# First tokens read once, later sums made tile by tile, and twelve sums of each stage on VectorE

## The chip, the core and the metric

The kernel runs on one core of a Trainium2 chip. The core has TensorE (PE in the profile; PEld is its weight load), VectorE (DVE), ScalarE (ACT), GpSimd (POOL) and SyncE (SP, which here only issues DMAs), each with its own queue of instructions that runs in order. The metric is the device time of one execution in microseconds (us), lower is better, as the median of several runs.

## The reference

One layer works on 1024 tokens of 1024 channels in float32: a feed-forward block (ffn1), a mixer (a short convolution beside a gated delta rule), a second feed-forward block (ffn2), a last norm. Each of the three blocks begins with the same two steps, an RMS norm and a wide matmul:

```python
def rmsnorm(x, w, eps=NORM_EPS):
    xf = x.astype(jnp.float32)
    y = xf * lax.rsqrt(jnp.mean(xf * xf, axis=-1, keepdims=True) + eps)
    return (y * w.astype(jnp.float32)).astype(x.dtype)
...
def swiglu_ffn(x, w_in, w_out):
    gate, up = jnp.split(x @ w_in, 2, axis=-1)
    return (jax.nn.silu(gate) * up) @ w_out
...
    h = h + 0.5 * swiglu_ffn(rmsnorm(h, ffn1_norm[layer]), ffn1_w_in[layer], ffn1_w_out[layer])
    u = rmsnorm(h, mix_norm[layer]) @ w_mix_in[layer]
```

## The kernel before

**Tiles.** The activations lie transposed, channels on the 128 partitions: `h[hf][d]` is a tile of 128 channels by 512 tokens, `hf` the half of the tokens (first, second) and `d` one of eight groups of channels. A product in float32 accuracy is three matmuls (`mm3`, L192 to L194): each operand is split into a high and a low part, and hi*hi, hi*lo and lo*hi are summed in PSUM. The high part is a copy on ACT (L103), the low part a subtraction on DVE (L104). For weights the parts are called `whi` and `wlo`, for activations `hi` and `lo`. One product of a 512x128 block of weights with a 512x512 block of activations is four `mm3`, so 12 matmuls of 512 columns.

**Strassen-Winograd.** A `Pair` takes two column blocks of a weight matrix, 2x2 blocks B11 to B22, against the 2x2 blocks A11, A12, A22 of the activations, in seven products in place of eight. That needs sums on both sides: of the weights, T1 = B12 - B11, T2 = T1 - B22, T3 = B22 - B12, T4 = B21 + T2 (`tsum`, `prep_p6`); of the activations, S1, nS2, S3, S4 (`Blocks.sums`, in three parts), for which the second half's tokens have to be normed. Before the change all T and the S4 were made on POOL through `pool_tt` (L111), the other S on DVE.

**The order at the start of a stage.** A stage here is the beginning of ffn1, of the mixer's projections (mix) or of ffn2. PE first does the "heads" of five early pairs: `head1` (B11 with A11), then `head2` (B21 with A12). These need the first half's tokens alone. Then come, for the first two pairs together, the products with S1 and nS2 (`both(k)`, k = 0 to 3: 2 pairs x 2 products x 3 = 12 matmuls for each k), then heads of later pairs between the products P7, P4 and P3. Work is given out as tasks of (load, prep, run), with loads 9 and preps 4 tasks ahead of the run (`run_tasks`); the framework's scheduler then orders DVE's instructions by its own plan, except those inside `keep_in_program_order`. `later(n, f)` calls f after n more `mm3`. `x.sums(0, ...)` made all four S1 and nS2 in one go, as soon as the second half's norm factor was spread (`spread`, a transpose on PE at L246 that puts one factor per token into all partitions).

**The beginning of ffn1.** `first_heads` read the tokens of the first half twice: as rows (`xtok`, 8 tiles of 256 KB, tokens on partitions), squared on ACT with a running sum for each token (`by_tokens`, L235), and as `xT` for the product. The factor is a power -0.5 on POOL (L220), which like the transposes needs the constants tile `cs`. `cs` was loaded on ACT's queue; `mask` (L783, L784) is cast from it on DVE. The second half was read as rows and as `xT` after that. The weights of the small projection `wba` were loaded and split at this point too (L745 to L749), though they are used only in the mixer.

Of the kernel before, what the change touches and what calls it, by code (L numbers as in the profile page):

```python
# [57 lines left out]
def tile_hybrid(  # L58
# [54 lines left out]


    tasks, done_to = [], [0, 0, 0]

# [39 lines left out]
    nc.scalar.activation(out=early, in_=early, func=AF.Square)  # L156

    ident = cs[:, C_ID:C_ID + P]
# [45 lines left out]
    class Norm:  # L204
# [24 lines left out]

        def by_tokens(self, src):  # L230

            tot = const.tile([P, 8], F32, name="tot", tag="tot", bufs=2)
            for i, tile_ in enumerate(src):
                tc.keep_in_program_order(
                    nc.scalar.activation(out=tile_, in_=tile_, func=AF.Square, accum_out=tot[:, i:i + 1]))  # L235
            tv = tot.rearrange("p (b i) -> p b i", i=2)
            both = const.tile([P, 4], F32, name="both", tag="both", bufs=2)
            nc.vector.tensor_tensor(out=both, in0=tv[:, :, 0], in1=tv[:, :, 1], op=ALU.add)
            self.factor(both)
# [28 lines left out]
    class Blocks:  # L268
# [3 lines left out]
        def __init__(self, h, which):  # L272
            self.h, self.g = h, V_N[which]
            self.s4 = []
            self.b = {n: [None] * KH for n in ("A11", "A12", "S1", "nS2", "S3", "S4", "A22")}
# [12 lines left out]
        def begin2(self, k):  # L288
# [5 lines left out]
                                           op0=ALU.mult, op1=ALU.add)  # L294

        def sums(self, part, rb):

            h, b = self.h, self.b
            if part == 0:
                for k in range(KH):  # L300
                    s1, s2 = h[1][k], h[0][k]
                    nc.vector.tensor_tensor(out=s1, in0=s1, in1=rb, op=ALU.mult)
                    nc.vector.tensor_tensor(out=s2, in0=s2, in1=s1, op=ALU.subtract)  # L303
                    b["S1"][k] = split(s1, slot)
                    b["nS2"][k] = split(s2, slot)
            if part == 1:
                for k in range(KH):
                    a22, s2 = h[1][k + KH], h[0][k]
                    nc.vector.scalar_tensor_tensor(out=a22, in0=a22, scalar=self.gain(k + KH), in1=rb,
                                                   op0=ALU.mult, op1=ALU.mult)  # L310
                    s4 = temp(F32, "s4")
                    self.s4.append(s4)
                    pool_tt(s4, h[0][k + KH], s2, ALU.add)
                    nc.vector.tensor_tensor(out=s2, in0=s2, in1=a22, op=ALU.add)
                    b["S3"][k] = split(s2, slot)
            if part == 2:
                for k in range(KH):
                    b["A22"][k] = split(h[1][k + KH], slot)
                for k in range(KH):
                    b["S4"][k] = split(self.s4[k], slot)  # L320

    class Pair:
# [5 lines left out]
        def __init__(self, x, srcs, first, done):  # L328
            self.x, self.srcs, self.first, self.done = x, srcs, first, done
            self.r, self.t, self.w, self.pinned = {}, {}, {}, False  # L330

# [48 lines left out]
        def body(self):  # L380
# [6 lines left out]
            def prep_p6():  # L387
                t["T1"] = tt_tile("T1")
                pool_tt(t["T1"], r["B12"], r["B11"], ALU.subtract)
                self.tsum("T2", t["T1"], r["B22"], ALU.subtract)  # L390
# [34 lines left out]
    def all_pairs(pairs, x, norm2, between={}, twos=(0, 2)):  # L425
# [214 lines left out]
    with ExitStack() as stack:  # L640
# [3 lines left out]

        def by_tokens(hf):
            tiles = []
            for b in range(KH):
                for i in range(2):
                    tiles.append(slot(F32, "xtok"))
                    tc.keep_in_program_order(nc.sync.dma_start(out=tiles[-1], in_=xtok[hf, b][:, i, :]))  # L650
            return tiles

        def get_x(hf, *ds):
# [3 lines left out]
        def first_heads(pairs):  # L657
            early = pairs[:EARLY]
            four = early[:4]
            for p in early:  # L660
                p.pinned = True
            rows1 = by_tokens(0)
            for k in range(KH):
                get_x(0, k)
                early[k].get("B11")
            get_x(0, *range(KH, KT))
            norms[0].by_tokens(rows1)
            norms[0].spread()
# [4 lines left out]
            def first(k):  # L673
                x.norm1(norms[0].rb, k)
                x.split1(k)

            def run(k):
# [3 lines left out]
                if k == KH - 1:  # L681
                    for p in four:
                        p.w.pop("B11")
                        p.copy_p1()

            for k in range(KH):
                first(k)
            rows2 = []

            def then():  # L690
                for d in range(KH, KT):
                    first(d)
                norms[1].by_tokens(rows2)

            def then2():
                for k in range(KH):
                    x.begin2(k)

            for k in range(KH):
                task(lambda k=k: run(k))  # L700
            task(*early[4].head1())
            task(*early[0].head2())
            task(None, then, lambda: rows2.extend(by_tokens(1)))
            task(*early[1].head2())
            task(None, None, lambda: get_x(1, 0, 4, 1, 5))
            task(*early[2].head2())
            task(norms[1].spread, then2, lambda: get_x(1, 2, 6, 3, 7))
            task(*early[3].head2())
            task(*early[4].head2())

# [5 lines left out]

        def t1_done():
            for d in range(KT):
                nm[0].square(d)
                nc.sync.dma_start(out=h_dr[0][d], in_=acc[0][d])  # L720
# [861 lines left out]
```

## Time and profile before

| | us |
|---|---|
| median of three runs (1858.66, 1865.97, 1868.80) | 1865.97 |
| the profiled execution's own time | 1864.1 |
| its span, first to last instruction | 1862.4 |
| granted TensorE clock over the span, share of full | 0.989 |

The page of the profile gives, for each engine, its busy time; a page's groups give line, engine, operation, output<-inputs, shapes, count, then busy time, mean length of one in ns, and the idle time before them with what ended it. In a timeline row stand the start, the length, the engine, the line, the operation and the tiles, and in brackets the idle time of that engine just before and what released it. In a row of windows stand the window, its length, each engine's busy time with the number of instructions that touch the window, the granted clock, the DMA engines' share and rate. An instruction on DVE is 0.68 us long in a timeline, but the next starts before its end.

### The profile page before, as it was taken

Reading aid. Unit: us, or ns where it says so; the run is one execution under the profiler, and the core shown is the slowest. Engines: PE = TensorE matmul, PEld = TensorE weight load, DVE = VectorE, ACT = ScalarE, POOL = GpSimd, SP = SyncE. Lnnn points to the kernel's source line nnn. Section 1 sums busy time; section 2 is a strip of 40 time slices with the busy share of each in tenths; the row PEclk is TensorE's granted clock in tenths of the full one; section 3 lists DMA queues with packets and bytes.
Section 4 is the critical chain, followed back from the end, with each engine's and each line's share of the span. In section 5 each row is a group of like instructions: output and inputs, shape, how many; then the busy total and the mean of one; then the engine's idle time right before and its main releaser. Section 6 shows DMA issues by size and latency. Waiting matters only on the chain.

```text
span 1862.4 us, 24801 instructions
## 1 busy us (share of the span) xinstructions
PE 1793.7 (96%) x8448; PEld 1464.3 (79%) x8448; DVE 1304.6 (70%) x1997; ACT 751.3 (40%) x1520; POOL 731.4 (39%) x514
## 2 busy tenths in 40 slices
PE   6899999999999999999989999999999999999997
PEld 4688888888888877777778887778888888888886
DVE  5976666667665887877867665878665666677666
ACT  6422323223534554468343344443222323244443
POOL 2474455445341432324322102045544454445243
PEclk9999999999999999999999999999999999999998
DMA  8144344435984542478744385522434344488642
GB/s 296 57 153 141 114 141 137 135 120 197 321 273 142 167 145 90 142 229 276 241 136 153 109 284 170 194 88 97 168 116 141 114 140 138 158 286 280 215 141 92
DMA packets 196238, 313.48 MB, mean 168 GB/s; under 512 B 28048, under 2 KB 50576, under 8 KB 196112
## 3 DMA queue, kind: packets, MB, share of 16 engines
q1 hardware_dynamic: 192656, 306.60, 49.9%
q10 hardware_dynamic: 3456, 5.31, 0.9%
q8 instruction: 66, 1.08, 0.2%
q14 instruction: 60, 0.49, 0.1%
HBM read 228.97 MB, written 82.86 MB: 167 GB/s over the span
## 4 chain that ended last, share of the span: by engine, by line
PE 78%; DVE 10%; ACT 4%; DMA 3%; issue 3%; POOL 1%; SPq 0%; ACTq 0%; POOLq 0%; DVEq 0%
PE ps_ps L194 22%; PE ps_ps L192 22%; PE ps_ps L193 22%; PE ps_mm L192 2%; PE ps_mm L194 2%; PE ps_mm L193 2%; DVE wlo L104 2%; DVE lo L104 1%; PE ps_aux L938 1%; DMA raw<-w_in 1%; DVE cv L842 1%; DVE sv L1092 1%; DVE xb L1096 1%; ACT whi L103 1%; DVE h L303 1%
## 5 line engine op out<-in xcount | busy, mean ns | idle before, releaser
L192 PE MATMUL ps_ps<-hi,whi 128*128 128x512 f32 x1400 | 550.1, 394 | 10.6 <-ACT hi L103 3.2
L194 PE MATMUL ps_ps<-hi,wlo 128*128 128x512 f32 x1400 | 548.5, 392 | 9.0 <-DVE wlo L104 9.0
L193 PE MATMUL ps_ps<-lo,whi 128*128 128x512 f32 x1400 | 549.0, 392 | 2.9 <-DVE lo L104 2.9
L104 DVE TENSOR_TENSOR wlo<-T,whi 128x512 fp32r<-128x512 f32 x244 | 228.8, 952 | 144.9 <-ACT whi L103 144.3
L104 DVE TENSOR_TENSOR wlo<-raw,whi 128x512 fp32r<-128x512 f32 x280 | 251.6, 909 | 102.3 <-ACT whi L103 100.5
L192 PEld LDWEIGHTS ps_ps<-hi,whi 128*128 128x128 f32 x1400 | 264.7, 189 | 72.0 <-ACT whi L103 4.7
L194 PEld LDWEIGHTS ps_ps<-hi,wlo 128*128 128x128 f32 x1400 | 264.9, 189 | 66.9 <-DVE wlo L104 11.7
L111 POOL TENSOR_TENSOR T<-raw 128x512 f32<-128x512 f32 x144 | 222.8, 1548 | 234.8 <-DVE wlo L104 102.5
L193 PEld LDWEIGHTS ps_ps<-lo,whi 128*128 128x128 f32 x1400 | 265.0, 189 | 60.3 <-DVE lo L104 5.6
L192 PE MATMUL ps_ps<-ghi,whi 128*128 128x512 f32 x616 | 241.3, 392 | 0.0
L194 PE MATMUL ps_ps<-ghi,wlo 128*128 128x512 f32 x616 | 240.8, 391 | 0.4 <-DVE wlo L104 0.4
L193 PE MATMUL ps_ps<-glo,whi 128*128 128x512 f32 x616 | 240.6, 391 | 0.0
L103 ACT CAST whi<-raw 128x512 fp32r<-128x512 f32 x280 | 169.2, 617 | 62.7 <-DMA raw<-w_in 23.0
L103 ACT CAST whi<-T 128x512 fp32r<-128x512 f32 x244 | 146.3, 616 | 76.1 <-PE ps_ps L193 33.1
L104 DVE TENSOR_TENSOR glo<-raw,ghi 128x512 fp32r<-128x512 f32 x154 | 128.7, 836 | 50.9 <-ACT ghi L103 48.2
L192 PE MATMUL ps_mm<-hi,whi 128*128 128x512 f32 x384 | 159.8, 416 | 3.8 <-ACT whi L103 2.7
L194 PE MATMUL ps_mm<-hi,wlo 128*128 128x512 f32 x384 | 152.7, 398 | 1.3 <-DVE wlo L104 1.3
L193 PE MATMUL ps_mm<-lo,whi 128*128 128x512 f32 x384 | 152.3, 397 | 0.0
L111 POOL TENSOR_TENSOR T<-raw,T 128x512 f32<-128x512 f32 x50 | 72.4, 1449 | 167.1 <-DMA raw<-w_in 127.5
L194 PEld LDWEIGHTS ps_ps<-ghi,wlo 128*128 128x128 f32 x616 | 115.7, 188 | 26.8 <-DVE wlo L104 1.3
L193 PEld LDWEIGHTS ps_ps<-glo,whi 128*128 128x128 f32 x616 | 115.9, 188 | 25.3
L192 PEld LDWEIGHTS ps_ps<-ghi,whi 128*128 128x128 f32 x616 | 115.7, 188 | 25.3
(223 smaller groups left out, 2230.7 us busy)
## 6 DMA issues: line engine op xcount, KB each, us to landing
raw<-w_in SPq DMA_DIRECT2D x264, 256.0 KB, 4.6
raw<-w_out SPq DMA_DIRECT2D x154, 256.0 KB, 4.2
raw<-w_qkv SPq DMA_DIRECT2D x36, 256.0 KB, 3.4
f1S<-S SPq DMA_DIRECT2D x33, 256.0 KB, 5.0
raw<-f1A SPq DMA_DIRECT2D x33, 256.0 KB, 3.9
raw<-f1S SPq DMA_DIRECT2D x33, 256.0 KB, 3.7
f2S<-S SPq DMA_DIRECT2D x33, 256.0 KB, 4.9
raw<-f2A SPq DMA_DIRECT2D x33, 256.0 KB, 4.4
```

Source lines behind the costliest of these rows:

```text
L103: tc.keep_in_program_order(nc.scalar.copy(out=hi, in_=src))
L104: nc.vector.tensor_tensor(out=lo, in0=src, in1=hi.bitcast(F32), op=ALU.subtract)
L111: tc.keep_in_program_order(nc.gpsimd.tensor_tensor(out=out, in0=in0, in1=in1, op=op))
L192: nc.tensor.matmul(out=ps, lhsT=whi, rhs=xhi, start=start, stop=False, skip_group_check=True)
L193: nc.tensor.matmul(out=ps, lhsT=whi, rhs=xlo, start=False, stop=False, skip_group_check=True)
L194: nc.tensor.matmul(out=ps, lhsT=wlo, rhs=xhi, start=False, stop=stop, skip_group_check=True)
L303: nc.vector.tensor_tensor(out=s2, in0=s2, in1=s1, op=ALU.subtract)
L842: nc.vector.scalar_tensor_tensor(out=acc, in0=u[:, i:i + HALF], scalar=vcol(wc + i), in1=acc, op0=ALU.mult, op1=ALU.add)
L938: nc.tensor.matmul(out=ps[:, sl], lhsT=lhs[:, sl], rhs=rhs[:, sl], start=start, stop=stop)
L1092: nc.vector.tensor_tensor(out=tv, in0=lrow[:, lo:hi].unsqueeze(2).broadcast_to([nb, n, j + 1]), in1=xrow[:, 0:j + 1].unsqueeze(1).broadcas ...
L1096: nc.vector.tensor_tensor(out=xv, in0=xv, in1=tv, op=ALU.subtract)
```

## The change

- `first_heads` loads the eight `xT` tiles of the first half first, then `cs` (now on SP's queue), then four weight blocks, the rows of the second half, its `xT` tiles, then the other weights. The rows of the first half aren't read at all.
- `as_they_land` takes the first half's sums from `xT`: ACT squares each tile, DVE adds two tiles at a time, PE sums over the channels by four matmuls with a column of ones, four times, into one PSUM bank.
- The second half's rows are squared one by one between the first half's splits (`row_square`), and its factor is spread right after the first 48 matmuls.
- `sums(0)` makes the first S1 and nS2, and gives the other three to `later` (4, 8 and 12 `mm3` on); `both(k)` asks for its own with `need(k)`.
- S4 in `sums(1)` and all T of the first two pairs go to DVE, in every stage: 4 + 8 sums of 128x512.
- `wba` is loaded and split at the end of ffn1's output product T1 (`split_ba`).

```diff
+    def dve_tt(out, in0, in1, op):
+        nc.vector.tensor_tensor(out=out, in0=in0, in1=in1, op=op)
...
     cs = const.tile([P, NCONST], F32, name="cs")
-    nc.scalar.dma_start(out=cs, in_=cst)
...
+        def as_they_land(self):
+
+            cp = psum(self.bank)
+            for j in range(KH):
+                two = [slot(F32, "sq") for _ in range(2)]
+                for i, sq in enumerate(two):
+                    tc.keep_in_program_order(
+                        nc.scalar.activation(out=sq, in_=self.hh[2 * j + i], func=AF.Square))
+                nc.vector.tensor_tensor(out=two[0], in0=two[0], in1=two[1], op=ALU.add)
+                for b in range(4):
+                    tc.keep_in_program_order(
+                        nc.tensor.matmul(out=cp[:, b:b + 1], lhsT=two[0][:, b * P:(b + 1) * P], rhs=one,
+                                         start=(j == 0 and b == 0), stop=(j == KH - 1), skip_group_check=True))
+            self.factor(cp[:, 0:4])
...
+        def need(self, k):
+            while self.b["S1"][k] is None:
+                self.pending.pop(0)()
...
             if part == 0:
-                for k in range(KH):
-                    s1, s2 = h[1][k], h[0][k]
...
+                self.pending = [lambda k=k: first(k) for k in range(KH)]
+                self.need(0)
+                for k in range(1, KH):
+                    later(SUM_STEP * k, lambda k=k: self.need(k))
...
-                    pool_tt(s4, h[0][k + KH], s2, ALU.add)
+                    nc.vector.tensor_tensor(out=s4, in0=h[0][k + KH], in1=s2, op=ALU.add)
...
-            pool_tt(self.t[n], p, q, op)
+            self.tt(self.t[n], p, q, op)
...
+        for p in pairs[:2]:
+            p.tt = dve_tt
...
-            rows1 = by_tokens(0)
-            for k in range(KH):
-                get_x(0, k)
-                early[k].get("B11")
-            get_x(0, *range(KH, KT))
-            norms[0].by_tokens(rows1)
+            get_x(0, *range(KT))
+            tc.keep_in_program_order(nc.sync.dma_start(out=cs, in_=cst))
+            for p in four:
+                p.get("B11")
+            rows2 = []
+            for b in range(KH):
+                for i in range(2):
+                    rows2.append(slot(F32, "xtok"))
+                    tc.keep_in_program_order(nc.sync.dma_start(out=rows2[-1], in_=xtok[b][:, i, :]))
+            norms[0].as_they_land()
```

What the change moves on DVE's queue shows at three places. The first is the very start, before: `tot` and `both` are the row sums, `ms` the mean square.

```order
L783 CAST mask_290<-cs_68 128x128
L784 CAST mask_290<-cs_68 128x128
L238 TENSOR_TENSOR both_229<-tot_220 128x4
L218 TENSOR_SCALAR ms_231<-both_229 128x4
L104 TENSOR_TENSOR wlo_242<-raw_205,whi_241 128x512
L282 SCALAR_TENSOR_TENSOR h_73<-h_73,vs_66,ps_ps_235 128x512
```

The same place in the changed kernel, with `ps_ps_222` the bank of the new sums:

```order
L812 CAST mask_318<-cs_68 128x128
L813 CAST mask_318<-cs_68 128x128
L243 TENSOR_TENSOR sq_223<-sq_223,sq_224 128x512
L243 TENSOR_TENSOR sq_232<-sq_232,sq_233 128x512
L243 TENSOR_TENSOR sq_241<-sq_241,sq_242 128x512
L243 TENSOR_TENSOR sq_250<-sq_250,sq_251 128x512
L105 TENSOR_TENSOR wlo_270<-raw_198,whi_269 128x512
L223 TENSOR_SCALAR ms_259<-ps_ps_222 128x4
```

The four additions stand behind both casts from `cs`, and `ms` behind all of them and one split of weights.

The second place is ffn1 between the second half's gains and the products `both`, before. L293 is the second half's gain, L302 makes S1 (`h_82`), L303 nS2; the T come from POOL and only their splits stand here.

```order
L293 SCALAR_TENSOR_TENSOR h_84<-h_88,vs_66,h_84 128x512
L104 TENSOR_TENSOR wlo_518<-raw_389,whi_517 128x512
L302 TENSOR_TENSOR h_81<-h_81,ps_ps_565 128x512
L104 TENSOR_TENSOR wlo_536<-raw_438,whi_535 128x512
L104 TENSOR_TENSOR wlo_544<-T2_541,whi_543 128x512
L104 TENSOR_TENSOR wlo_562<-T1_539,whi_561 128x512
```

In the changed kernel, some way behind the same gains, the T of the first two pairs are made on DVE between the sums:

```order
L117 TENSOR_TENSOR T1_567<-raw_429,raw_427 128x512
L328 TENSOR_TENSOR h_85<-h_85,ps_ps_495 128x512
L105 TENSOR_TENSOR lo_562<-h_76,hi_561 128x512
L117 TENSOR_TENSOR T2_569<-T1_567,raw_431 128x512
L329 TENSOR_TENSOR h_77<-h_77,h_85 128x512
L117 TENSOR_TENSOR T1_617<-raw_467,raw_465 128x512
L105 TENSOR_TENSOR wlo_572<-T2_569,whi_571 128x512
L105 TENSOR_TENSOR lo_590<-h_85,hi_589 128x512
L105 TENSOR_TENSOR wlo_600<-T1_567,whi_599 128x512
L105 TENSOR_TENSOR lo_594<-h_77,hi_593 128x512
L117 TENSOR_TENSOR T2_619<-T1_617,raw_469 128x512
```

The split of the first T1 (`wlo_562`, `wlo_600`) is the 5th instruction behind the last gain before the change, with all but one of the S1 and nS2 behind it; after the change it is the 26th, with all S1 and nS2 and the heads' last weights ahead of it.

The third place is the mixer's start, before. `raw_6047`, `raw_6081` and `raw_6087` are the weights of the third, fourth and fifth `head2`; the spread factor is used first 10 rows ahead of this piece.

```order
L302 TENSOR_TENSOR h_4498<-h_4498,ps_ps_6159 128x512
L104 TENSOR_TENSOR lo_6188<-h_4468,hi_6187 128x512
L303 TENSOR_TENSOR h_4218<-h_4218,h_4498 128x512
L104 TENSOR_TENSOR lo_6192<-h_4186,hi_6191 128x512
L104 TENSOR_TENSOR wlo_6214<-raw_6047,whi_6213 128x512
L104 TENSOR_TENSOR lo_6198<-h_4498,hi_6197 128x512
L104 TENSOR_TENSOR wlo_6233<-raw_6081,whi_6232 128x512
L104 TENSOR_TENSOR lo_6202<-h_4218,hi_6201 128x512
L104 TENSOR_TENSOR wlo_6252<-raw_6087,whi_6251 128x512
```

After: `raw_6059`, `raw_6093` and `raw_6099` are the same three weights, and `h_4411` is the first S1, the first use of the factor.

```order
L117 TENSOR_TENSOR T1_6281<-raw_6122,raw_6120 128x512
L328 TENSOR_TENSOR h_4411<-h_4411,ps_ps_6171 128x512
L105 TENSOR_TENSOR wlo_6196<-raw_6059,whi_6195 128x512
L329 TENSOR_TENSOR h_4120<-h_4120,h_4411 128x512
L105 TENSOR_TENSOR lo_6180<-h_4411,hi_6179 128x512
L328 TENSOR_TENSOR h_4437<-h_4437,ps_ps_6171 128x512
L105 TENSOR_TENSOR lo_6184<-h_4120,hi_6183 128x512
L329 TENSOR_TENSOR h_4151<-h_4151,h_4437 128x512
L105 TENSOR_TENSOR lo_6215<-h_4437,hi_6214 128x512
L105 TENSOR_TENSOR wlo_6225<-raw_6093,whi_6224 128x512
L105 TENSOR_TENSOR lo_6219<-h_4151,hi_6218 128x512
L328 TENSOR_TENSOR h_4475<-h_4475,ps_ps_6171 128x512
```

The three weights' low parts were 15th, 17th and 19th from the first use of the factor; they are 2nd, 9th and 12th (`raw_6099` follows the last row shown). In ffn2 they move in the same way.

More of the change, by code (lines that the diff above doesn't have):

```diff
@@ L156, in tile_hybrid @@
     nc.scalar.activation(out=early, in_=early, func=AF.Square)
+    one = const.tile([P, 1], F32, name="one")
+    nc.vector.memset(one, 1.0)
     ident = cs[:, C_ID:C_ID + P]
@@ L228, in reduce, with row_square, by_rows @@
             self.factor(cp[:, 0:4])
[L230 to L237, printed above, removed]
+        def as_they_land(self):
[11 more added lines that the diff above has]
+            self.factor(cp[:, 0:4])
+        def row_square(self, i, tile_):
+            if i == 0:
+                self.tot = const.tile([P, 8], F32, name="tot")
+            tc.keep_in_program_order(
+                nc.scalar.activation(out=tile_, in_=tile_, func=AF.Square, accum_out=self.tot[:, i:i + 1]))
+        def by_rows(self):
+            tv = self.tot.rearrange("p (b i) -> p b i", i=2)
+            both = const.tile([P, 4], F32, name="both")
             nc.vector.tensor_tensor(out=both, in0=tv[:, :, 0], in1=tv[:, :, 1], op=ALU.add)
@@ L294, in begin2, with first @@
                                            op0=ALU.mult, op1=ALU.add)
+        def need(self, k):
+            while self.b["S1"][k] is None:
+                self.pending.pop(0)()
         def sums(self, part, rb):
             h, b = self.h, self.b
-            if part == 0:
-                for k in range(KH):
-                    s1, s2 = h[1][k], h[0][k]
[L302 to L305, printed above, removed]
+            def first(k):
+                s1, s2 = h[1][k], h[0][k]
+                nc.vector.tensor_tensor(out=s1, in0=s1, in1=rb, op=ALU.mult)
+                nc.vector.tensor_tensor(out=s2, in0=s2, in1=s1, op=ALU.subtract)
+                b["S1"][k] = split(s1, slot)
+                b["nS2"][k] = split(s2, slot)
+            if part == 0:
+                self.pending = [lambda k=k: first(k) for k in range(KH)]
+                self.need(0)
+                for k in range(1, KH):
+                    later(SUM_STEP * k, lambda k=k: self.need(k))
             if part == 1:
@@ L370, in both @@
                 self.z, self.y = psum(), psum()
+            self.x.need(k)
             ks = slice(k * P, (k + 1) * P)
@@ L643, in tile_hybrid @@
         norms = [Norm(h[hf]) for hf in range(NH)]
[L645 to L651, printed above, removed]
         def get_x(hf, *ds):
@@ L684, in run @@
                         p.copy_p1()
+                    norms[1].spread()
             for k in range(KH):
                 first(k)
-            rows2 = []
             def then():
@@ L692, in then @@
                     first(d)
-                norms[1].by_tokens(rows2)
-            def then2():
+                norms[1].by_rows()
                 for k in range(KH):
                     x.begin2(k)
-            for k in range(KH):
+            task(lambda: run(0), then, lambda: get_x(1, 0, 4, 1, 5, 2, 6, 3, 7))
+            for k in range(1, KH):
                 task(lambda k=k: run(k))
             task(*early[4].head1())
[L702 to L709, printed above, removed]
+            for p in early:
+                task(*p.head2())
         g_dr = ffn_in(x, norms, w1_in, "f1", first_heads)
@@ L1556 @@
         "xT": a["x"][0].T.reshape(KT, P, NH, HALF).transpose(2, 0, 1, 3),
-        "xtok": a["x"][0].reshape(NH, KH, P, 2, HALF),
+        "xtok": a["x"][0][HALF:].reshape(KH, P, 2, HALF),
         "w1_in": w_in(a["ffn1_w_in"][0]),
```

20 lines of the change are left out of this document (12 added, 8 removed).

## The prediction

> **What bounds the kernel now.** First the page's busy times, then PE's waits:
>
> ```profile
> PE 1793.7 (96%) x8448; PEld 1464.3 (79%) x8448; DVE 1304.6 (70%) x1997; ACT 751.3 (40%) x1520; POOL 731.4 (39%) x514
> ...
> PE ps_ps L246 <- POOL rs L220: 12.6, 1, 12.6
> PE ps_ps L194 <- DVE wlo L104: 9.3, 6, 3.8
> ```
>
> PE is the bound, so only time in which PE stands still, or runs slowly, can be won. Two of its waits belong to places that the change touches: the first factor, and the low parts of weights that DVE delivers late. I then looked at how many matmuls pass in a stretch. These rows give PE's pace, and two waits in mix and ffn2:
>
> ```profile
> 67.07 0.39 PE L194 MATMUL ps_ps<-hi,wlo 128*128 128x512 f32 x1
> 67.75 0.39 PE L194 MATMUL ps_ps<-hi,wlo 128*128 128x512 f32 x1
> 23.60 0.63 PE L192 MATMUL ps_ps<-hi,whi 128*128 128x512 f32 x1
> 24.03 0.45 PE L193 MATMUL ps_ps<-lo,whi 128*128 128x512 f32 x1
> 692.89 0.60 PE L194 MATMUL ps_ps<-hi,wlo 128*128 128x512 f32 x1 [3.82 <-DVE wlo L104]
> 1229.89 0.79 PE L194 MATMUL ps_ps<-hi,wlo 128*128 128x512 f32 x1 [3.22 <-DVE wlo L104]
> ```
>
> The first two are three matmuls apart: 0.68/3 = 0.227 us each at full pace. The next two are neighbours at 0.43, the pace at the start and for some ten matmuls after each long wait. Now windows of PE, cut where products begin:
>
> ```profile
> 24.03:49.32 25.29, 24.87 (x111) 1.00 0.65 234
> 49.32:65.03 15.71, 12.63 (x50) 1.00 0.14 44
> 65.03:92.41 27.38, 24.24 (x98) 0.94 0.20 62
> 688.46:702.32 13.86, 10.04 (x38) 0.88 0.18 57
> 1226.06:1240.51 14.45, 11.23 (x37) 0.76 0.17 54
> ```
>
> The counts take in what touches the edges; by the code 106, 48, 96, 36 and 36 matmuls start in them. At 0.227 they need 24.1, 10.9, 21.8, 8.2 and 8.2 us. **Lost: 1.2, 4.8, 5.6, 5.7 and 6.3 us.** The second window is `both` in ffn1, the third the eight products after it, the last two are three heads in mix and in ffn2, where the third `head2` waits for its `wlo`.
>
> Why DVE is late there:
>
> ```profile
> 38.94:69.10 30.16, 25.70 (x107) 18.71 (x105) 30.16 (x40) 15.39 (x27) 12.98 (x8) 1.00 0.22 71
> 53.12 0.68 DVE L104 TENSOR_TENSOR lo<-h,hi 128x512 fp32r<-128x512 f32 x1
> 53.72 0.67 DVE L302 TENSOR_TENSOR h<-h,ps_ps 128x512 f32<-128x512 f32 x1
> 54.31 1.17 DVE L104 TENSOR_TENSOR lo<-h,hi 128x512 fp32r<-128x512 f32 x1
> 53.27 1.66 POOL L111 TENSOR_TENSOR s<-h 128x512 f32<-128x512 f32 x1 [1.23 <-DVE h L303]
> ```
>
> DVE (third busy time) has no gap in 30.16 us. An instruction takes 0.60 us of its queue (53.12 to 53.72), but a `lo` beside a sum on POOL took 1.17. And the stretch begins late, behind ACT:
>
> ```profile
> 36.10 1.28 ACT L472 ACT_TABLE_LOAD   x1
> 38.19 2.55 ACT L292 ACTIVATE h<-h,vs 128x512 f32<-128x512 f32 x4
> ```
>
> The second half's gains on ACT start only after the first heads' Silu.
>
> **The front.** The rows of before:
>
> ```profile
> 9.65 0.63 ACT L235 ACTIVATE xtok<-xtok 128x512 f32<-128x512 f32 x1
> 10.33 0.63 ACT L235 ACTIVATE xtok<-xtok 128x512 f32<-128x512 f32 x1
> 5.50 0.23 DVE L783 CAST mask<-cs 128x128 fp32r<-128x128 f32 x1 [4.57 <-DMA cs<-cst]
> 5.65 0.22 DVE L784 CAST mask<-cs 128x128 fp32r<-128x128 f32 x1
> 614.60 0.79 PE ps_ps L226 x8
> 11.28 0.17 DVE L218 TENSOR_SCALAR ms<-both 128x4 f32<-128x4 f32 x1
> 13.75 1.41 DVE L282 SCALAR_TENSOR_TENSOR h<-h,vs,ps_ps 128x512 f32<-128x512 f32 x2 [0.72 <-PE ps_ps L246]
> 16.28 2.17 ACT L103 CAST hi<-h 128x512 fp32r<-128x512 f32 x4
> 16.94 1.65 PE L192 MATMUL ps_ps<-hi,whi 128*128 128x512 f32 x3 [3.23 <-ACT hi L103]
> 19.59 0.80 PE L193 MATMUL ps_ps<-lo,whi 128*128 128x512 f32 x1 [1.00 <-DVE lo L104]
> ```
>
> Dropping eight tiles looks like a gain of some 5 us (8 at 0.68, the spacing of the first two rows). It isn't, because the added wait stands at the head of DVE's queue: the casts from `cs`, with four additions, a weight split and `ms` behind them. Before, eight tiles and `cs` had landed by 10.33; now the same bytes come with `cs` last, so the casts start at about 10.3. They take 0.37, the additions 3 x 0.60 + 0.68 = 2.5, the last four PE sums half of 0.79, with latency `ms` starts at 13.7. From `ms` to the normed tile took 13.75 - 11.28 = 2.47: 16.2, which is 2.4 later than before. ACT gives part back: it reached the first `hi` only at 16.28, busy with weight casts; now those are done, `hi` follows the first tile (0.74 long) at 17.0 and the product 0.66 behind it, **at 17.6 against 16.94**. The low part needs three tiles and one split: 18.9 against 19.59, so PE runs through. Full pace came 4.44 us after PE ran without a break (19.59 to 24.03); from 17.6 that is 22.0 with 10 matmuls done, and the 14th, at 24.03 before, starts at 22.8: **1.2 us won.** `cs` may land at 9.6 (nine tiles at 0.68 from 4.2) or a microsecond late, so -0.5 to 2.2. By the Trainium skill (TensorE: Matmul & The Clock Gate, What's actually happening) a free-running window of about 3.4 us decides, which would put full pace near 21.0 and the gain at 1.7, but the trace's 4.44 is used.
>
> **The heads and `both` in ffn1.** ACT now takes `hi` and row squares in turn, 0.54 and about 0.61 each, so eight of both end at 26.5. The second half's gains follow directly, with DVE's from 27.2 instead of 38.94. Four gains and four weight splits reach 32.2, and 22 instructions to the first T1 split make 13.2 at 0.60: 45.4. PE reaches `both` at 22.8 + 24.1 + 0.4 for the spread = 47.3. The second pair's T are wanted 1.8 to 3.2 us after that, and their high parts wait on ACT behind the fifth head's Silu, which PE releases only at 47.3: margins of half a microsecond to two. So I count the whole 4.8 of `both` and 0.6 of the 1.2 ahead of it. In the third window the two waits that I look at are these:
>
> ```profile
> 69.91 0.47 PE L192 MATMUL ps_ps<-hi,whi 128*128 128x512 f32 x1 [1.78 <-DVE u L378]
> 84.32 0.50 PE L192 MATMUL ps_ps<-hi,whi 128*128 128x512 f32 x1 [0.96 <-ACT p L352]
> ```
>
> The first, and the slow matmuls behind it, come from DVE's backlog and go; of the second, which hangs on the S4 splits, I keep 0.6. So 5.0 of 5.6.
>
> **Mix and ffn2.** The third `head2`'s weight stood behind nearly all S1 and nS2 and comes 13 places earlier on DVE (2nd in place of 15th), the other two 8 and 7. In mix, with the factor out at 678.4, they are ready by 679.6, 683.8 and 685.6; PE wants them at 688.5, 691.2 and 693.9. `both` is then wanted at 688.46 + 8.2 = 696.6, and the T's last split is the 28th from the factor, near 695.5. So the wait goes, and the slow matmuls with it: 5.7 and, in the same way, 6.3.
>
> **What the moved sums cost.** Each stage puts 12 more instructions on DVE. The nearest row for their length, and what POOL took and cost:
>
> ```profile
> L303 DVE TENSOR_TENSOR h<-h 128x512 f32<-128x512 f32 x4 | 2.7, 678 | 0.0
> L111 POOL TENSOR_TENSOR s<-h 128x512 f32<-128x512 f32 x4 | 6.7, 1674 | 7.9 <-DVE h L303 7.9
> 678.36:695.17 16.81, 12.99 (x54) 10.30 (x53) 16.81 (x20) 9.56 (x19) 10.88 (x12) 0.94 0.18 61
> 1215.35:1232.83 17.48, 14.26 (x57) 11.37 (x56) 17.48 (x21) 10.94 (x19) 10.57 (x7) 0.89 0.21 67
> ```
>
> 12 x 0.60 = 7.2 us added. Against it, DVE was delayed: 20 instructions in mix's 16.81 us and 21 in ffn2's 17.48 need 12.1 and 12.7 at 0.60, and the 40 in ffn1's 30.16 need 24.1. About 6.1, 4.7 and 4.8 go if POOL is quiet there. So 1 to 2.5 net for each stage, hidden under PE while the margins hold; at worst 7.2 each, at best a gain where only T1 and T2, four sums or 2.4 us, stand ahead of `both`. `wba` leaves the front, and its new place costs nothing: its DVE work lands where DVE waits on ACT.
>
> ```profile
> 594.44 0.69 DVE L104 TENSOR_TENSOR wlo<-T,whi 128x512 fp32r<-128x512 f32 x1 [1.45 <-ACT whi L103]
> ```
>
> **The sum**: 1.2 + 0.6 + 4.8 + 5.0 + 5.7 + 6.3 = 23.6. For margins this thin I charge 2.0 in new small waits: 21.6. From the profiled execution's 1864.1 that is 1842.5; the three runs of before have their median 1.9 higher, so I say 1843.
>
> **The rivals.**
>
> *DVE stays the bound.* POOL's share of the delay may be small, with sums slowed on DVE itself. The Trainium skill speaks for that (Perfetto Trace Analysis, Optimizing Scalar/DVE Operations): GpSimd and VectorE share a read port, so moving operations between the two might not help. For it in this trace: DVE had no gap. Against it: instructions that read PSUM, such as 53.72 beside POOL's 53.27, keep 0.67, so the delay does come from POOL. With the rest of the delay kept, T would come some 5 us later in mix and ffn2 and the waits reappear at `both`; 11.6 in ffn1 less 2 remain, 1864.1 - 9.6 = 1854. Chance 0.17.
>
> *The gain is lost on the way.* PE also waits between 780 and 980, with the DMA engines full:
>
> ```profile
> 820.00:840.00 20.00, 19.35 (x108) 16.33 (x107) 15.08 (x23) 19.63 (x42) 11.87 (x9) 1.00 0.94 292
> ```
>
> If transfers there pace the stage by themselves, the 17.3 won ahead of it are lost and ffn2's 6.3 stay: 1858. Against it: those DMAs wait for data made just before. Chance 0.09.
>
> *Slower.* One mechanism: DVE's in-order queue at `both`. If the spacing gives nothing, each wait only moves, and DVE carries 7.2 more in three places, 21.6, with at most 6.1 + 4.7 + 4.8 of relief: 1864.1 + 6.0 = 1870, and 1886 with none. It decides from the point where DVE delivers later than PE's arrival plus the old waits (4.8, 5.7, 6.3): more than 7 us beyond my times. Chance 0.06. That the rows aren't dropped is no rival: SP's queue has eight loads fewer.
>
> **How the numbers follow.** Forecast 0.68, at 1836 to 1850. The range reaches up to 1857, which takes in the first rival: about 0.83. Half a per cent, what a measurement of this kernel can tell from no change, is 1856.6: faster 0.68 + 0.13 = 0.81; slower (over 1875) 0.04; the rest 0.15.
>
> **What would show it.** First product at 17.6 behind casts from `cs` at 10.3; DVE's gains near 27; `both` in 11 to 12 us; three heads of mix and ffn2 in 8.2; PE's wait for `wlo` under 3 in all; POOL 36 instructions fewer; splits at 0.68 in these stretches. I am wrong if PE waits for T splits at `both`, or if the gain at 100 us isn't some 11.

## The result and the profile after

| | before | after |
|---|---|---|
| median, us (four runs each) | 1865.10 | 1849.04 |
| lowest and highest, us | 1858.66, 1868.80 | 1845.63, 1850.12 |
| profiled execution, us | 1864.1 | 1848.53 |
| its span, us | 1862.4 | 1846.4 |

The ratio is 0.9924, 95% interval [0.9907, 0.9941]: faster by 0.76%, 16 us. The forecast was 1843, with 1836 to 1850 as the likely times and a range up to 1857.

First the line of busy times on the page of the changed kernel; the bound is still PE, and GpSimd has 478 instructions, the 36 fewer that were forecast:

```profile
PE 1790.4 (97%) x8480; PEld 1466.6 (79%) x8480; DVE 1307.3 (71%) x2037; ACT 751.5 (41%) x1512; POOL 674.6 (37%) x478
```

Then the list of PE's waits (total, times, longest). The 9.3 us for `wlo` and the 12.6 for the first factor are gone; PE's first wait is now for the squares' additions, and a wait for `p` has grown:

```profile
PE ps_ps L246 <- DVE sq L243: 11.6, 1, 11.6
...
PE ps_ps L197 <- ACT p L384: 3.0, 2, 2.3
...
PE ps_ps L268 <- POOL rs L225: 1.7, 1, 1.7
```

The five stretches of the prediction, cut at the same matmuls as before (window, its length, PE's busy time and instructions, granted clock, DMA share, GB/s):

```profile
28.45:52.95 24.50, 24.50 (x111) 1.00 0.27 88
52.95:64.03 11.08, 11.08 (x50) 1.00 0.14 47
64.03:88.53 24.50, 22.23 (x97) 1.00 0.22 76
683.81:691.97 8.16, 8.16 (x37) 1.00 0.10 32
1216.30:1224.46 8.16, 8.16 (x38) 1.00 0.11 35
```

The second column against that of before: 25.29 - 24.50 = 0.8 won in the heads, 15.71 - 11.08 = 4.6 in `both`, 27.38 - 24.50 = 2.9 in the eight products, 13.86 - 8.16 = 5.7 in mix, 14.45 - 8.16 = 6.3 in ffn2. That is 20.3. But the 14th matmul starts at 28.45, and before at 24.03: the front **loses 4.4**. 20.3 - 4.4 = 15.9, and the spans differ by 16.0: these six terms make up the difference. Elsewhere the two kernels drift by 1.0 us at most in a stretch, both ways, and that cancels.

The front and the wait for `p` in the timeline of the changed kernel:

```profile
10.58 0.23 DVE L812 CAST mask<-cs 128x128 fp32r<-128x128 f32 x1 [9.62 <-DMA cs<-cst]
10.72 0.22 DVE L813 CAST mask<-cs 128x128 fp32r<-128x128 f32 x1
10.86 2.49 DVE L243 TENSOR_TENSOR sq<-sq 128x512 f32<-128x512 f32 x4
...
11.60 6.99 PE L246 MATMUL ps_ps<-one,sq 128*128 128x1 f32 x32 [11.60 <-DVE sq L243]
...
18.62 0.16 DVE L223 TENSOR_SCALAR ms<-ps_ps 128x4 f32<-128x4 f32 x1 [4.67 <-PE ps_ps L246]
18.86 1.40 POOL L225 TENSOR_TENSOR rs<-ms,cs 128x4 f32<-128x4 f32 x1 [16.58 <-DVE ms L223]
...
22.92 0.79 PE L197 MATMUL ps_ps<-hi,whi 128*128 128x512 f32 x1 [1.49 <-ACT hi L104]
...
28.21 0.41 PE L197 MATMUL ps_ps<-hi,whi 128*128 128x512 f32 x1
...
32.08 2.74 DVE L315 SCALAR_TENSOR_TENSOR h<-h,vs 128x512 f32<-128x512 f32 x4 [0.16 <-ACT h L314]
...
80.46 0.50 PE L197 MATMUL ps_ps<-hi,whi 128*128 128x512 f32 x1 [2.27 <-ACT p L384]
```

Read the first three rows as a queue: DVE stands 9.62 us for `cs`, makes two casts that nobody needs before the mixer, and only then the four additions. So PE's sums, 16 matmuls in the code and 32 on the engine (each is done in two), all begin after 11.5 and run one behind the other for 6.99 us. `ms` starts at 18.62.

### The profile page after: what moved, and what is told of

The parts are those of the page before. It is cut to its first block, busy times and chain, and to the rows that moved or that the text cites. A ratio compares the mean times of both kernels' runs of the same rounds, so it can differ in the third digit from the quotient of the medians.

```text
span 1846.4 us, 24832 instructions
## 1 busy us (share of the span) xinstructions
PE 1790.4 (97%) x8480; PEld 1466.6 (79%) x8480; DVE 1307.3 (71%) x2037; ACT 751.5 (41%) x1512; POOL 674.6 (37%) x478
## 4 chain that ended last, share of the span: by engine, by line
PE 82%; DVE 7%; DMA 4%; ACT 3%; issue 2%; POOL 1%; SPq 0%; ACTq 0%; POOLq 0%; DVEq 0%
PE ps_ps L197 24%; PE ps_ps L199 24%; PE ps_ps L198 23%; PE ps_mm L197 2%; PE ps_mm L199 2%; PE ps_mm L198 2%; DVE cv L871 1%; PE ps_aux L967 1%; DVE wlo L105 1%; DVE sv L1121 1%; DVE xb L1125 1%; DMA raw<-w_in 1%; DVE lo L105 1%; PE ps_aux L993 0%; ACT whi L104 0%
## 5 line engine op out<-in xcount | busy, mean ns | idle before, releaser
L112 POOL TENSOR_TENSOR T<-raw 128x512 f32<-128x512 f32 x132 | 205.0, 1554 | 306.5 <-DVE wlo L105 108.3
L105 DVE TENSOR_TENSOR wlo<-raw,whi 128x512 fp32r<-128x512 f32 x280 | 242.8, 878 | 98.9 <-ACT whi L104 97.6
L384 ACT COPY p<-ps_ps 128x512 f32<-128x512 f32 x50 | 29.0, 586 | 241.9 <-PE ps_ps L199 235.4
```

The lines of the kernel that those rows point to most:

```text
L105: nc.vector.tensor_tensor(out=lo, in0=src, in1=hi.bitcast(F32), op=ALU.subtract)
L112: tc.keep_in_program_order(nc.gpsimd.tensor_tensor(out=out, in0=in0, in1=in1, op=op))
L384: ins = nc.scalar.copy(out=self.p1[:, 3:HALF + 3], in_=self.x_ps)
```

## The experiments

Each ratio is to the kernel before on the same chip; the spans are of one profiled execution.

| run | ratio, 95% interval | span, us | first product, us |
|---|---|---|---|
| changed kernel, first time | 0.9924 [0.9907, 0.9941] | 1846.4 | 22.92 |
| e1_mask_late | 0.9905 [0.9885, 0.9924] | 1840.6 | 17.50 |
| e2_cs_early | 0.9911 [0.9890, 0.9932] | 1843.0 | 17.98 |
| e3_sums_dve | 0.9925 [0.9904, 0.9947] | 1843.9 | 21.70 |
| e5_mask_temps | 0.9904 [0.9885, 0.9922] | 1841.2 | 17.52 |
| e0_after_again | 0.9938 [0.9920, 0.9956] | 1847.0 | 22.65 |
| e4_front_only | 1.0039 [1.0026, 1.0053] | 1865.9 | 22.46 |
| e6_pool_sums | 0.9992 [0.9980, 1.0004] | 1852.5 | 22.26 |
| e7_no_space | 0.9919 [0.9899, 0.9940] | 1840.0 | 22.00 |
| e8_best | 0.9890 [0.9870, 0.9909] | 1835.7 | 18.05 |
| e10_warm | 0.9878 [0.9865, 0.9892] | 1836.5 | 17.76 |
| e12_s4_pool | 0.9948 [0.9929, 0.9967] | 1847.2 | 17.80 |
| e11_before_dve | 0.9949 [0.9933, 0.9964] | 1851.8 | 17.56 |

### The front: who holds it up

**e1_mask_late.** The two casts go from the head of VectorE's queue to ScalarE, into `split_ba`:

```diff
-        nc.vector.tensor_copy(out=mask[:, 0:P], in_=gt)
-        nc.vector.tensor_copy(out=mask[:, P:2 * P], in_=ones)
...
+            tc.keep_in_program_order(nc.scalar.copy(out=mask[:, 0:P], in_=gt))
+            tc.keep_in_program_order(nc.scalar.copy(out=mask[:, P:2 * P], in_=ones))
```

> The changed kernel with the two mask casts taken off the head of VectorE's queue: they are made on ScalarE, much later, and nothing else is edited. Theory A (the front is late because the casts wait for cs, the four additions wait behind the casts, and so all 32 small matmuls of the sums, 0.21 us each, run one behind the other from 11.60 to 18.59): the additions now follow their tiles from about 5 us, three quarters of the sums lie beside the landing, the last 8 cost 1.7, ms starts at about 13.0 in place of 18.62, and the first product at 17.3 (17.0 to 17.8) in place of 22.92. Time 1849.0 - 5.6 = 1843.4. Rival B (the sums themselves or the landing of cs set the start, wherever the casts stand): first product at 21 or later, time within 1.5 of 1849. Rival C (the start comes early, but the gain is lost at the first wait behind it): first product near 17.3, gain under 2 at the 200th product.

The timeline of e1_mask_late:

```profile
5.09 0.69 DVE L243 TENSOR_TENSOR sq<-sq 128x512 f32<-128x512 f32 x1 [4.13 <-ACT sq L242]
...
5.84 1.87 PE L246 MATMUL ps_ps<-one,sq 128*128 128x1 f32 x8 [5.84 <-DVE sq L243]
...
7.88 5.28 PE L246 MATMUL ps_ps<-one,sq 128*128 128x1 f32 x24 [0.17 <-DVE sq L243]
...
13.20 0.16 DVE L223 TENSOR_SCALAR ms<-ps_ps 128x4 f32<-128x4 f32 x1 [1.38 <-PE ps_ps L246]
...
75.03 0.50 PE L197 MATMUL ps_ps<-hi,whi 128*128 128x512 f32 x1 [2.48 <-ACT p L384]
```

Theory A holds closely: `ms` at 13.20 (13.0 expected), the first product at 17.50 (17.3). Most of the sums now lie beside the landing of the tiles, though not all that I counted: the last 24 run without a break, so PE is the limit here too, from 7.88 on. The span is 5.8 under that of the changed kernel. The intervals of the two ratios overlap, so the medians alone don't show the gain; the row at 17.50 does.

**e2_cs_early.** `cs` is loaded early and the casts stay:

```diff
     cs = const.tile([P, NCONST], F32, name="cs")
+    nc.scalar.dma_start(out=cs, in_=cst)
...
-            tc.keep_in_program_order(nc.sync.dma_start(out=cs, in_=cst))
```

> The changed kernel with cs loaded second on ScalarE's queue, as before the change, in place of last behind the eight tiles; the casts stay where they are. Theory A: the casts run near 5.5 and hold nothing up, the tiles land up to 0.7 us later for the bytes of cs ahead of them; first product at 17.3 + 0.7 = 18.0, time 1844.1. Rival B (not the casts' wait): first product at 22 to 23.6, time 1849 to 1850.

The timeline of e2_cs_early:

```profile
5.28 0.23 DVE L812 CAST mask<-cs 128x128 fp32r<-128x128 f32 x1 [4.31 <-DMA cs<-cst]
...
6.48 7.16 PE L247 MATMUL ps_ps<-one,sq 128*128 128x1 f32 x32 [6.48 <-DVE sq L244]
...
13.68 0.16 DVE L224 TENSOR_SCALAR ms<-ps_ps 128x4 f32<-128x4 f32 x1 [1.95 <-PE ps_ps L247]
...
17.98 0.80 PE L198 MATMUL ps_ps<-hi,whi 128*128 128x512 f32 x1 [1.49 <-ACT hi L104]
```

17.98, where 18.0 was expected. A second remedy for the same wait gives about the same start, so what counts is the wait for `cs` and not the place of the casts.

**e3_sums_dve.** The casts stay where they are; the squares are added up to one tile, and PE does 4 sums in place of 16:

```diff
+                if j > 0:
+                    nc.vector.tensor_tensor(out=two[0], in0=two[0], in1=last, op=ALU.add)
+                last = two[0]
...
-                        nc.tensor.matmul(out=cp[:, b:b + 1], lhsT=two[0][:, b * P:(b + 1) * P], rhs=one,
+                    nc.tensor.matmul(out=cp[:, b:b + 1], lhsT=last[:, b * P:(b + 1) * P], rhs=one,
...
```

> The changed kernel with the casts left at the head of the queue, and the four sums of two squares added up to one tile on VectorE (three additions more), so that TensorE has 8 small matmuls in place of 32. Theory A: the additions run from 10.86 for 7 x 0.60 and a split between them, to about 15.7; 8 matmuls at 0.21 are 1.7; ms at 17.5, 1.1 ahead of the 18.62 of the changed kernel; first product at 21.8, time 1848. If the matmuls' number were all that matters, and not that they start late: ms at 11.6 + 1.9 = 13.5, first product at 17.8, time 1844. If their number doesn't matter: ms at 18.6 or later, time 1849 or more.

The timeline of e3_sums_dve:

```profile
10.01 0.23 DVE L815 CAST mask<-cs 128x128 fp32r<-128x128 f32 x1 [9.05 <-DMA cs<-cst]
...
15.49 1.87 PE L249 MATMUL ps_ps<-one,sq 128*128 128x1 f32 x8 [15.49 <-DVE sq L245]
...
17.40 0.16 DVE L223 TENSOR_SCALAR ms<-ps_ps 128x4 f32<-128x4 f32 x1 [1.36 <-PE ps_ps L249]
```

Expected 17.5, measured 17.40, but 0.57 of the 1.2 won is `cs`, which landed earlier in this execution (casts at 10.01 against 10.58). A quarter of the matmuls helps little while the additions start so late. Late start and price go together: the 4 sums are 8 matmuls on the engine, which take 1.87 us here, and 0.79 in the row at 614.60 on which the prediction's price rests.

**e5_mask_temps** is e1_mask_late with 21 temporary tiles:

```diff
-TEMPS = 20
+TEMPS = 21
```

> e1_mask_late with 21 temporary tiles in place of 20. In the changed kernel TensorE waits 2.4 us at 80.46 for the copy p, which ScalarE starts only when VectorE has split the first S4 sum and so given up its tile. Theory D (the copy waits for a free temporary tile): one tile more takes most of this wait away, 1.5 to 2.4 us, and the time is 1843.4 - 1.8 = 1841.6. Rival E (the copy stands behind ScalarE's queue or VectorE's, whatever tiles there are): the wait stays at over 2 us, time 1843.4.

The timeline of e5_mask_temps:

```profile
73.66 0.50 PE L197 MATMUL ps_ps<-hi,whi 128*128 128x512 f32 x1 [0.68 <-ACT p L384]
...
142.10 0.50 PE L197 MATMUL ps_ps<-hi,whi 128*128 128x512 f32 x1 [0.60 <-DVE c L439]
```

Theory D holds for the wait: 2.48 becomes 0.68. The gain isn't kept. After 240 matmuls e5 is 1.4 ahead of e1 (76.52 and 77.92), after 600 it is 0.5 behind (160.38 and 159.91), in part through small waits for VectorE that e1 hasn't, the one at 142.10 among them; the spans are 1841.2 and 1840.6. VectorE has as much to do as before, so it may be that one more tile only lets PE meet it elsewhere; no run shows that.

### Which edit wins the rest

**e0_after_again** is the changed kernel, beside the next three.

> The changed kernel itself, beside the three that follow and the kernel before on one chip. Every theory expects its ratio to be that of its first measurement, 0.9924 within [0.9907, 0.9941], its first product at 22.9 and its span within 3 of 1846.4.

0.9938, first product at 22.65, span 1847.0: as the first time.

**e4_front_only** is the changed kernel with both edits that follow the beginning undone:

```diff
-            p.tt = dve_tt
+            p.tt = pool_tt
...
-                    nc.vector.tensor_tensor(out=s4, in0=h[0][k + KH], in1=s2, op=ALU.add)
+                    pool_tt(s4, h[0][k + KH], s2, ALU.add)
...
-                    later(SUM_STEP * k, lambda k=k: self.need(k))
+                    self.need(k)
```

> The changed kernel with T1, T2 and S4 sums put back on GpSimd and the second tokens' first sums made in one go: of the change only the new beginning (loads, sums of squares, order of the early heads) is left. Theory (the beginning loses 4.7, and of the gain in ffn1 only a part is due to it; mix and ffn2 owe their 12 us to the two other edits): the 4.7 are lost at the 48th product, some 4 to 5 are won between the 84th and the 240th, and nothing in mix and ffn2, where the waits of 3.8 and 3.2 for the third head's wlo are back: span 1862 (1859 to 1864), about that of before. Rival (the early gains of the second half do all of ffn1's): 9 us won from the 84th to the 240th, span 1858.

The timeline of e4_front_only:

```profile
50.45 0.61 ACT L104 CAST whi<-raw 128x512 fp32r<-128x512 f32 x1
...
51.11 0.50 PE L197 MATMUL ps_ps<-hi,whi 128*128 128x512 f32 x1 [3.58 <-ACT whi L104]
...
54.43 1.28 DVE L105 TENSOR_TENSOR wlo<-raw,whi 128x512 fp32r<-128x512 f32 x2
...
55.16 0.80 PE L199 MATMUL ps_ps<-hi,wlo 128*128 128x512 f32 x1 [1.83 <-DVE wlo L105]
```

Slower than before, and by more than expected: the 4.3 of the start are lost (after 48 matmuls, 36.38 against 32.06), and PE waits 3.6 and 1.8. These waits aren't for T: the splits that end just before, on ACT and on VectorE, are `whi<-raw` and `wlo<-raw`, of weights of the heads ahead of `both`. `both` itself passes in 10.88 (61.21 to 72.09), where it took 15.71 before. So the early gains take the wait away from `both`, and it stands at the heads instead. I had counted 4 to 5 won between 84 matmuls and 240; it was 1.9. In mix and ffn2 nothing is won.

**e6_pool_sums** undoes only the move of the sums (the first two pieces of that diff).

> The changed kernel with the T1, T2 and S4 sums back on GpSimd; the spacing of the second tokens' first sums stays. Theory (both edits are needed: the spacing brings wlo in time, the quiet GpSimd brings T in time): the three heads of mix and ffn2 still pass in 8.2 us each, but the splits of S1, nS2 and T take 0.8 us and more beside GpSimd, and TensorE waits for T at both, 3 us or more in mix and in ffn2 and 1 to 4 in ffn1: span 1846.4 + 9 = 1855 (1853 to 1859). Rival (the spacing alone does it): no such wait, span 1846 to 1848.

The timeline of e6_pool_sums, a place in mix, and one wait each in mix and ffn2:

```profile
678.02 1.69 POOL L112 TENSOR_TENSOR T<-raw 128x512 f32<-128x512 f32 x1 [1.23 <-DMA raw<-w_qkv]
678.47 0.67 DVE L328 TENSOR_TENSOR h<-h,ps_ps 128x512 f32<-128x512 f32 x1
679.07 1.19 DVE L105 TENSOR_TENSOR lo<-h,hi 128x512 fp32r<-128x512 f32 x1
680.07 1.33 POOL L112 TENSOR_TENSOR T<-T,raw 128x512 f32<-128x512 f32 x1 [0.36 <-DMA raw<-w_qkv]
680.18 1.77 DVE L329 TENSOR_TENSOR h<-h 128x512 f32<-128x512 f32 x1
...
698.08 0.50 PE L199 MATMUL ps_ps<-hi,wlo 128*128 128x512 f32 x1 [2.19 <-DVE wlo L105]
...
1232.60 0.50 PE L199 MATMUL ps_ps<-hi,wlo 128*128 128x512 f32 x1 [1.51 <-DVE wlo L105]
```

The heads of mix and ffn2 pass without a wait, and the wait is at `both` instead, 2.2 and 1.5 for a split of T, less than the 3 expected. Beside a sum on GpSimd, VectorE's instruction with both inputs in SBUF takes 1.19 and 1.77, and the one that reads PSUM keeps 0.67. The Trainium skill (SBUF — State Buffer, Who interferes with whom) says that a VectorE instruction with two SBUF inputs contends with a GpSimd instruction that reads SBUF, and one with at most one such input doesn't; these rows agree.

**e7_no_space** undoes only the spacing (the last piece).

> The changed kernel with the second tokens' first sums made in one go, as before the change; T1, T2 and S4 stay on VectorE. Theory (both edits are needed): the third head's wlo stands behind S1 and nS2 again, 13 places later, 7.8 us at 0.60; of the relief from GpSimd some 3 us come off, so TensorE waits 2 to 4 us for it in mix and in ffn2, and with the slow matmuls behind such a wait 4 to 5.5 us are lost in each: span 1846.4 + 9.5 = 1856 (1853 to 1858). Rival (the moved sums alone do it, since VectorE's instructions then take 0.60): no wait over 1 us there, span 1846 to 1848.

Windows of e7_no_space: the three heads of mix and of ffn2 on PE, then mix's stretch of VectorE with all engines (PE, PEld, DVE, ACT, POOL in this order, then clock, DMA share, GB/s):

```profile
682.74:690.90 8.16, 8.16 (x37) 1.00 0.40 129
1210.99:1219.15 8.16, 8.16 (x38) 1.00 0.33 114
...
672.62:686.21 13.59, 13.59 (x62) 11.22 (x61) 13.38 (x23) 9.68 (x20) 0.00 (x0) 1.00 0.29 95
```

My theory that both edits are needed falls. Without the spacing, mix and ffn2 take the same 8.16. The last row tells why: with GpSimd silent, 23 instructions of VectorE take 13.59 us, 0.59 each; before, 20 took 16.81, 0.84 each. The rival given beside it stands. The span, 1840.0, is even 6 under the rival's 1846 to 1848, but not through this edit: 1.7 are there by the 14th matmul, where the front is the same, and 4.2 arise between matmuls 3000 and 4000, where the two kernels don't differ.

### The two remedies in one, and single sums

**e8_best** joins e1_mask_late and e7_no_space (the two diffs above, nothing else).

> e1_mask_late and e7_no_space in one: the mask casts off VectorE's queue, the sums of the second tokens in one go, T and S4 sums on VectorE. If the two parts add up: first product at 17.5, no wait over 1 us in mix and ffn2, span 1840.0 - 4.5 = 1835.5 (1833 to 1839), time some 22 us under that of the kernel before on the same chip (ratio 0.988). If the early start is lost again at the first both (VectorE's T sums not ready when TensorE arrives 4.5 earlier): a wait of 2 to 4.5 us there, span 1838 to 1840, ratio 0.990 to 0.992.

The span is 1835.7 (1835.5 expected), the ratio 0.9890, and the interval lies below that of the changed kernel in its second measurement, [0.9920, 0.9956]. The front's part adds up: the span is 4.3 under that of e7_no_space, 3.7 of it by the 14th matmul. That the whole sum comes out is partly luck. Of the 4.9 by which the span is under that of e1_mask_late, 4.2 arise between matmuls 3000 and 4000, where the two don't differ, and the intervals of these two ratios overlap.

**e12_s4_pool** is e8_best with the S4 sums on GpSimd:

```diff
-                    nc.vector.tensor_tensor(out=s4, in0=h[0][k + KH], in1=s2, op=ALU.add)
+                    pool_tt(s4, h[0][k + KH], s2, ALU.add)
```

> e8_best with only the S4 sums back on GpSimd; T1 and T2 stay on VectorE. Theory (each sum on GpSimd holds up VectorE's instructions beside it by 0.5 to 1.1 us; in mix before the change 2.2 us of the 5.4 lay beside T sums and 3.2 beside S4 sums): VectorE has instructions of 1.2 to 1.8 us again in mix and in ffn2, and the third head's wlo comes 2 to 3 us later; without the spacing it meets TensorE, so a wait of 0.5 to 1.5 us is back and 2 to 3.5 us are lost in each stage: span 5 over that of e8_best (2 to 8). Rival (T is what counts): same as e8_best within 1.

The timeline of e12_s4_pool in mix:

```profile
674.25 1.62 POOL L112 TENSOR_TENSOR s<-h 128x512 f32<-128x512 f32 x1 [3.22 <-DVE h L329]
674.62 1.79 DVE L329 TENSOR_TENSOR h<-h 128x512 f32<-128x512 f32 x1
...
684.57 0.50 PE L199 MATMUL ps_ps<-hi,wlo 128*128 128x512 f32 x1 [1.67 <-DVE wlo L105]
```

The wait for `wlo` is back, 1.7 in mix, by the S4 sums alone, four in each stage. The whole costs 11.5 against e8_best, more than the 2 to 8 expected: 4.5 are lost after 168 matmuls (63.91 and 59.39), 2.0 more in mix, 1.3 in ffn2, and 4.4 in the mixer between 3000 matmuls and 4000, where no edit is. Without that part it is 7, within what was expected.

**e11_before_dve** puts the moved sums alone into the kernel before:

```diff
...
+        for p in pairs[:2]:
+            p.tt = dve_tt
         norm2.then(lambda: x.sums(0, norm2.rb))
...
-                    pool_tt(s4, h[0][k + KH], s2, ALU.add)
+                    nc.vector.tensor_tensor(out=s4, in0=h[0][k + KH], in1=s2, op=ALU.add)
```

> The kernel before with a single edit: the first two pairs' T1 and T2 and the S4 sums on VectorE. The beginning and the sums in one go are those of before. Theory (after e7_no_space: GpSimd's sums were what held VectorE up, and no reordering is needed): mix and ffn2 are won in full, 5.7 and 6.3; in ffn1 the wait at both shrinks too, by 3 to 6; the first product stays at 16.9: span 1862.4 - 16 = 1846 (1843 to 1850). Rival (ffn1 needs the early gains: with them missing VectorE has 24 us of work and eight sums more ahead of both): ffn1 loses 2 to 5 more, span 1852 to 1855.

Windows of e11_before_dve, the heads of mix and ffn2, and behind them a row of its timeline in ffn1:

```profile
687.89:696.05 8.16, 8.16 (x37) 1.00 0.39 129
1221.61:1229.77 8.16, 8.16 (x37) 1.00 0.35 117
```

```profile
71.15 0.50 PE L195 MATMUL ps_ps<-hi,whi 128*128 128x512 f32 x1 [4.04 <-DVE u L381]
```

Both stages are won in full by this one edit. In ffn1 the rival is right: at the end of `both` the kernel is 1.0 ahead of before (64.00 against 65.03), but the wait for `u` behind it grows from 1.78 to 4.04, and nothing is left. Span 1851.8, and the rival said 1852 to 1855.

**e10_warm** gives PE wide work ahead of the first product of e8_best:

```diff
-            norms[0].spread()
...
+                        nc.tensor.matmul(out=junk, lhsT=w[:, 0:P], rhs=w, start=True, stop=True))
...
+            turn(4)
+            norms[0].spread()
+            turn(3)
```

The wide matmuls use the first split weights, so the spread now stands behind these splits in the code.

> e8_best with seven 512-column matmuls more on TensorE ahead of the first product, four before the spread and three behind it; their sums go to a bank that nobody reads. In e1_mask_late 24 matmuls of one column ran from 7.88 to 13.16 at 0.21 apart, and the products behind them still began at 0.43 and came to full pace 4.8 us later. Theory F (only wide matmuls bring the pace up, and standing still for 1.5 us in between sets it back): TensorE is at wide work from 13.2, full pace comes 4.4 to 5.3 us later, at 17.6 to 18.5, so the 14th product starts 1.5 to 2.2 us earlier, and the span is some 1.9 less. Rival G (full pace needs the real products, or the extra matmuls delay the spread and the first hi by as much): the 14th product within 0.5 of that of e8_best.

The timeline of e10_warm, then that of e8_best, both with the 13th product as the last row:

```profile
13.28 0.77 PE L708 MATMUL ps_ps<-whi 128*128 128x512 f32 x1
...
17.76 1.59 PE L197 MATMUL ps_ps<-hi,whi 128*128 128x512 f32 x4 [0.21 <-ACT hi L104]
...
21.03 0.39 PE L197 MATMUL ps_ps<-hi,whi 128*128 128x512 f32 x1
```

```profile
22.80 0.39 PE L197 MATMUL ps_ps<-hi,whi 128*128 128x512 f32 x1
```

Theory F: the 13th product starts 1.77 earlier, and so does the 14th; full pace comes at 18.73, a little behind the 17.6 to 18.5 expected. After 108, 0.3 of it is left: at splits of the heads' weights (`whi<-raw`, `wlo<-raw`) PE waits 0.3 and 0.7, where e8_best waits 0.4. The medians (1839.36 and 1842.78) have overlapping intervals, so whether the whole gains is open. It is the fastest kernel measured, and its interval lies below both of the changed kernel's.

## Why the prediction was right, and where it was wrong

**Direction and size.** Faster, as forecast; 1849.0 against 1843, inside the range. By its own sign the working was wrong all the same: the gain at 100 us should have been some 11, and it was 3.9. The three windows with the largest gains came out as worked out: `both` 4.6 (4.8 forecast), mix 5.7 (5.7), ffn2 6.3 (6.3), and the heads 0.8 (0.6).

**The front is the step that failed.** The prediction saw that the casts at the head of VectorE's queue hold up the additions, and placed them right (10.3, measured 10.58). It then let "the last four PE sums" cost "half of 0.79". Three things in that are wrong. Not four sums were behind the additions but all 16, since the first addition was itself behind the casts. The 8 matmuls of the row are four sums, each done in two, so four cost the whole 0.79 and not half. And in that row PE ran at full pace, 0.11 apart; at the start they are 0.21 apart. 0.4 became 6.99 us, and `ms` came at 18.62, not 13.7: 4.9 late. `rs` took 1.40, not the 1.01 of before, and the run-up to full pace a little longer, so the 14th matmul starts at 28.45, not 22.8. e1_mask_late and e2_cs_early show the cause by taking the wait away in two ways. With that wait gone the rest of the working nearly comes out in the trace: in e1_mask_late the 14th matmul starts at 22.77, and the same six terms are 1.3, 0.8, 4.6, 2.6, 5.7 and 6.3, together 21.3, where the sum said 21.6. The medians on that chip, 1859.99 and 1842.73, are 17.3 apart.

**The eight products behind `both`**: the right place and too large, 2.9 for 5.0. The wait for `u` went; the second, for `p`, grew from 0.96 to 2.27, where I had kept 0.6. It hangs on a temporary tile that the first S4 sum gives up (e5_mask_temps). The late front and this account for 5.6 + 2.1 of the 11.6 that the terms up to there add up to; 3.9 were left. The 2.0 charged for new small waits happens to be the size of the second shortfall, so the total is off by about the front's 5.6.

**Mix and ffn2: right numbers, half of the reason wrong.** The prediction gave two causes, `wlo` 13 places earlier and VectorE no longer held up. The second is enough: e7_no_space and e11_before_dve win the same 5.7 and 6.3 without the first. The prediction's own figures said so: 4.7 us of relief in mix against a wait of 3.82. With GpSimd still adding, the spacing does help (e6_pool_sums 0.9992, e4_front_only 1.0039); with the sums moved, none of its effect can be told (e0_after_again 0.9938, e7_no_space 0.9919, overlapping).

**In ffn1** neither part does it alone: the early gains without the moved sums leave waits of 3.6 and 1.8 at the heads (e4_front_only), the moved sums without the early gains a wait of 4.04 behind `both` (e11_before_dve). VectorE's gains of the second half started at 32.08, not 27: late by the front's 5, and still in time.

**The rivals.** That VectorE stays the bound: its mechanism is real, as e6_pool_sums shows, but needs GpSimd beside it. The page that spoke for it (the Trainium skill, Perfetto Trace Analysis, Optimizing Scalar/DVE Operations: moving work between GpSimd and VectorE might not help) isn't borne out here: one such move alone gives 0.9949 [0.9933, 0.9964]. The gain wasn't lost between 780 and 980: it was 10.3 after 3000 matmuls and 9.8 after 4000. Nor did VectorE's in-order queue turn it to slower.

**Open.** From 3000 matmuls to 4000, where no edit is, e8_best and e7_no_space take 340.7 and 341.2 us, the changed kernel 345.3 and the other runs 342.6 to 346.6. Part of that shows in the traces. PE waits there for loads of `gd` from `qkv_dr`: 3.7 in the changed kernel, 1.2 in e8_best, 0.8 in e7_no_space. And from 3600 to 3800 the granted clock is 0.94 in the changed kernel and 0.96 in e8_best. Why loads and clock differ isn't shown, so some 4 us between two spans say nothing of an edit. No run moves `wba` alone, and why `rs` takes 1.40 and not 1.01 wasn't tried.

## What to carry to other kernels

When an instruction that waits for a load is found at the head of an in-order queue, count everything behind it on the other engines too, down to the last one that could have been done meanwhile, and price it at the pace of that place, not from a row of the steady state. Where VectorE is late, look first at what GpSimd does beside it: moving a sum to VectorE costs 0.6 us there and can give back 1.1. When two edits are both said to cure a wait, check whether one of them covers it by its own figures; the other may only add risk.

## What the runs showed of the hardware

- **Narrow matmuls don't bring PE up to pace.** 32 one-column matmuls ran back to back for 6.99 us (0.21 apart from the first to the last), and the products behind them, after pauses of 1.73 and 1.49, still began at 0.43. With seven 512-column matmuls from 13.28 on, full pace was there at 18.73, 5.4 us later, through a pause. The Trainium skill (TensorE: Matmul & The Clock Gate, What's actually happening) tells of a window of about 3.4 us of activity; here the narrow ones ran for twice that and don't seem to count.
- **The run-up varies**: from the first product to full pace it took 5.3 us in the changed kernel (22.92 to 28.21) and 3.6 in e7_no_space (22.00 to 25.58), whose front is the same. The 14th product came 5.5 and 4.8 behind the first. A difference of 1 us at the start says nothing of an edit.
